# Moving seven of 31 convolution taps and the head norms' roots from VectorE to ScalarE and GpSimd in a hybrid decoder block

## The chip, the cores and the metric

The kernel runs on one core of a Trainium2 chip. The metric is the device time of one execution in microseconds (us), the median of several runs. A core has a matrix engine (TensorE, PE in the profile; its weight loads are PEld), a vector engine (VectorE, DVE), an activation engine (ScalarE, ACT), a general engine (GpSimd, POOL) and a queue that only starts transfers (SyncE, SP). Each engine works through its own list of instructions strictly in order and waits at semaphores for the others. SBUF is the working memory, PSUM the memory into which TensorE writes; GpSimd has no instruction here that touches PSUM.

## The reference, cut to what matters

One decoder layer over 512 tokens of width 1024, all in float32. Two token mixers run side by side on the same normed input, then comes an MLP:

```python
u = rms_norm(x, norm_mix_g)
proj = u @ w_in                          # q, k, v, glu (2 x 1024), two gates
q = rms_norm(q, q_norm_g) * HEAD_DIM ** -0.5      # 16 heads of 64
k = rms_norm(k, k_norm_g)                         # 4 heads of 64
attn = sliding_window_attention(q, k, v, attn_sinks, rel_bias) @ w_attn_o
h = a * sigmoid(gate)                    # the two halves of glu
h = causal_depthwise_conv(h, w_dw) + b_dw         # 31 taps, per channel
conv = silu(layer_norm(h)) @ w_conv_out
x = x + (sigmoid(gate_attn) * attn + sigmoid(gate_conv) * conv) @ w_out
x = x + square(relu(rms_norm(x, norm_mlp_g) @ w_ff1)) @ w_ff2
```

The window is 128 tokens, so a block of 128 queries sees its own and the previous block of keys. The convolution adds, for each of the 1024 channels, 31 shifted copies of a row of 512 tokens, each times a weight of that channel.

## The kernel before, in words

**Matrix products.** Every float32 product is made of three products of rounded halves: a matrix is split into a high part (ScalarE writes a rounded copy, `wh`, line 140) and a low part (the rest, `wl`, line 141). For the weights of the first half of the kernel GpSimd makes the low part, 128x1024 elements at a time.

**The stretch with the mixers.** `gemms()` (line 568) yields 80 steps: four times eight steps of `glu_pair` (the gate and value halves of the convolution input, lines 431 to 444, two tiles of 128 channels each) and four of `q_group` (the queries of four heads, line 473), then 32 steps for the two gates (`gates`, line 557). A step is one half of a weight tile's matrix products, or one block of 128 tokens of a query group. Between the steps a hand-written table (`stages`, lines 575 to 589) calls the attention pieces: `q_stage` transposes the scaled queries, `score_stage` makes the scores of four heads and their softmax, `prob_stage` transposes the probabilities, `value_stage` multiplies them with the values. The loop at line 598 also takes three convolution instructions per step from step 8 on (`CONV_STEP`, line 602); what is left at the end follows at line 614.

**Who orders.** Outside a short start the framework lists the instructions of each engine itself before the run: it goes by the order in which the program names them, and lets a later one pass when, by its own estimate of durations, an earlier one would still have to wait. On the chip that list is fixed.

**The convolution.** `conv_pair(c)` (line 446) works on two channel tiles. Their sums lie in two PSUM tiles (`cps`, tile name `cv`). All 31 taps of both are VectorE instructions on 128x512 elements: the first a product (line 455), the other 30 a product and a sum into the PSUM tile (line 457). Then VectorE adds the tile with its bias into `csum` (lines 463 and 465), and for the first three pairs ScalarE copies it out to SBUF with the bias (line 467). There are eight tiles, so 248 taps.

**The roots.** `q_group` copies the query block out of PSUM (ScalarE, line 258), squares it (line 260) and sums the squares of each head (VectorE, line 261). When its four blocks are done, `mean_eps` (line 131) and `rsqrt` (line 105) take 1/sqrt of 16 numbers per partition in 12 small VectorE instructions (lines 133, 110, 111 and three rounds of 113, 114 and 115). Line 486 then scales the queries on VectorE (both inputs in SBUF), line 487 rounds them on ScalarE, line 488 makes the low part on GpSimd, and only then can `q_stage` transpose them (line 498). The keys go the same way once, at the start (lines 401 to 416).

**What the attention pieces share.** `qtp` (line 496), `ptp` (line 535) and `op` (line 545) are PSUM tiles of one kind with two buffers, so TensorE can only write the next one when its readers are done with the one before the last: line 499 on ScalarE for `qtp`, 538 on ScalarE and 539 on VectorE for `ptp`, 552 on ScalarE and 554 on VectorE for `op`. Line 508 puts the sink column into the score tile on VectorE; line 518 adds the bias and takes the row minimum of the negated scores on VectorE; line 521 is the exponential on ScalarE; line 524 the reciprocal on VectorE; line 525 the scaling on GpSimd.

**After the stretch.** The low part of the attention output (`aTl`, line 612), the output projection with the layer norm of the convolution between its steps, the convolution's and the merged output projections, and the MLP, whose weights VectorE splits instead of GpSimd.

Of the kernel before, what the change touches and what calls it, by code (L numbers as in the profile page):

```python
# [42 lines left out]
START_ENGINES = {ENG.PE, ENG.DVE, ENG.Activation, ENG.Pool}  # L43
CONV_STEP = 3
LINE = 256
LEAD = 128
# [5 lines left out]
def tile_hybrid_block(  # L52
# [69 lines left out]
    def rsqrt_root(y, ms, w, tag):  # L122

        a = sm.tile([P, w], F32, name=f"a_{tag}", tag=f"a{w}")
        ve.reciprocal(y, y)
        ve.tensor_tensor(out=a, in0=y, in1=y, op=ALU.mult)
        ve.scalar_tensor_tensor(out=a, in0=a, scalar=-0.5, in1=ms, op0=ALU.mult, op1=ALU.mult)
        ve.scalar_tensor_tensor(out=y, in0=a, scalar=1.5, in1=y, op0=ALU.add, op1=ALU.mult)
        return y

# [269 lines left out]

    rk = rsqrt(mean_eps(ssk, HD, 16, "k"), 16, "k")
    k3 = kraw.rearrange("p t (g d) -> p (t g) d", d=HD)
# [28 lines left out]
    def glu_pair(c):  # L431
# [7 lines left out]
        for j, (wh, wl) in enumerate(stationary_tiles(w_in, V_END + 256 * c, 2, f"a{c}")):  # L439
# [4 lines left out]
                                    op0=ALU.add, op1=ALU.mult)  # L444

    def conv_pair(c):

        cts = (2 * c, 2 * c + 1)
        for ct in cts:
            cps[ct] = aux.tile([P, S], F32, name=f"cv_{ct}", tag="aux")  # L450
        for j in range(CW):
            for ct in cts:
                src, w = hh[ct][:, j:j + S], wcol[:, ct, j:j + 1]
                if j == 0:
                    ve.tensor_scalar(out=cps[ct], in0=src, scalar1=w, scalar2=None, op0=ALU.mult)
                else:
                    ve.scalar_tensor_tensor(out=cps[ct], in0=src, scalar=w, in1=cps[ct],  # L457
                                            op0=ALU.mult, op1=ALU.add)
                yield
        for ct in cts:  # L460
            b = wcol[:, ct, CW:CW + 1]
# [11 lines left out]
    def q_group(g):  # L473
# [3 lines left out]
        for t in range(NT):  # L477
# [23 lines left out]
    def score_stage(g, t):  # L501
# [5 lines left out]
        l4 = sm.tile([P, GRP], F32, name=f"l_{nm}", tag="l4")  # L507
        ve.tensor_copy(s4[:, :, 2 * P], nsink[:, GRP * g:GRP * g + GRP])
        for hp in range(2):
# [81 lines left out]
    def convs():  # L591
        for c in range(4):
            yield from conv_pair(c)

    conv = convs()
    last_stage = max(stages)
    ln = None
    for step, _ in enumerate(gemms()):
        for fn, args in stages.pop(step, []):
            fn(*args)  # L600
        if step >= 8:
            for _ in range(CONV_STEP):
                next(conv, None)
        if step == last_stage:
# [361 lines left out]
```

## Time and profile before

| | |
|---|---|
| time, median of 3 runs (lowest to highest) | 805.65 us (805.05 to 805.86) |
| the profiled execution's own time | 808.36 us |
| its span, from the first to the last instruction | 806.6 us |
| mean granted TensorE clock | 0.989 |
| DMA: moved, mean rate | 79.57 MB, 99 GB/s |
| the mixers' stretch, from the first convolution tap to the low part of the attention output | about 62 to 335 us of the span |

Times in the profile are microseconds from the start of the span unless marked ns. A row of groups has the line of the kernel, the engine, the operation, the tile it writes and those it reads, the shape, the count, then the busy time in all and the mean of one in ns, then the idle time in front. A row of waits reads "who waited, for whom: us in total, times, longest". A row of stretches has busy microseconds and instructions of each engine, then the granted TensorE clock as a share of full speed. Matrix products are pipelined, so their durations overlap and a busy TensorE is not one at its peak.

### The profile page before, as it was taken

Reading aid. Unit: us, or ns where it says so; the run is one execution under the profiler, and the core shown is the slowest. Engines: PE = TensorE matmul, PEld = TensorE weight load, DVE = VectorE, ACT = ScalarE, POOL = GpSimd, SP = SyncE. Lnnn points to the kernel's source line nnn. Section 1 sums busy time; section 2 is a strip of 40 time slices with the busy share of each in tenths; the row PEclk is TensorE's granted clock in tenths of the full one; section 3 lists DMA queues with packets and bytes.
Section 4 is the critical chain, followed back from the end, with each engine's and each line's share of the span. In section 5 each row is a group of like instructions: output and inputs, shape, how many; then the busy total and the mean of one; then the engine's idle time right before and its main releaser. Section 6 shows DMA issues by size and latency. Waiting matters only on the chain.

```text
span 806.6 us, 10416 instructions
## 1 busy us (share of the span) xinstructions
PE 781.7 (97%) x3960; PEld 662.8 (82%) x3960; DVE 629.4 (78%) x1046; ACT 378.8 (47%) x627; POOL 210.5 (26%) x108
## 2 busy tenths in 40 slices
PE   7999898998989999999999999999999999999998
PEld 7989796987968888787788889888888888888886
DVE  5539999999999999977983587687568756885683
ACT  5543255456565555244433436543554356435541
POOL 4343536344454443372357100000000000000000
PEclk8999999999999999999999999999999999999999
DMA  7421313213122213523134443333332332331002
GB/s 268 135 81 53 104 54 104 79 55 116 51 69 88 96 53 105 167 95 105 47 110 129 159 157 106 104 105 105 105 104 105 105 105 88 112 114 53 19 34 105
DMA packets 64808, 79.57 MB, mean 99 GB/s; under 512 B 2980, under 2 KB 52180, under 8 KB 64758
## 3 DMA queue, kind: packets, MB, share of 16 engines
q1 hardware_dynamic: 64758, 78.91, 29.7%
q8 instruction: 31, 0.51, 0.3%
q14 instruction: 19, 0.16, 0.1%
HBM read 76.78 MB, written 2.12 MB: 98 GB/s over the span
## 4 chain that ended last, share of the span: by engine, by line
PE 81%; DVE 14%; DMA 2%; issue 1%; POOL 1%; ACT 1%; SPq 0%; DVEq 0%; POOLq 0%; ACTq 0%
PE ps_f L175 7%; PE ps_f L176 7%; PE ps_f L174 7%; DVE cv L457 4%; PE ps_x L886 4%; PE ps_x L887 4%; PE ps_x L884 4%; PE ps_tc L422 2%; PE ps_tc L423 2%; PE ps_wo L182 2%; PE ps_wo L180 2%; PE ps_y L886 2%; PE ps_y L887 2%; PE ps_y L884 2%; PE ps_wo L181 2%; PE ps_tc L424 2%
## 5 line engine op out<-in xcount | busy, mean ns | idle before, releaser
L457 DVE SCALAR_TENSOR_TENSOR cv<-h,wcol,cv 128x512 f32<-128x512 f32 x240 | 167.2, 745 | 0.2
L175 PE MATMUL ps_f<-x2Tl,wh_f 128*128 128x512 f32 (+1 forms) x280 | 104.3, 373 | 0.4 <-DVE x2Tl L193 0.3
L174 PE MATMUL ps_f<-x2Th,wh_f 128*128 128x512 f32 (+1 forms) x280 | 103.7, 372 | 0.2 <-ACT x2Th L192 0.2
L176 PE MATMUL ps_f<-x2Th,wl_f 128*128 128x512 f32 (+1 forms) x280 | 103.9, 371 | 0.0
L141 DVE TENSOR_TENSOR wl_f<-raw_f,wh_f 128x1024 fp32r<-128x1024 f32 x32 | 39.1, 1224 | 57.8 <-ACT wh_f L140 56.6
L175 PEld LDWEIGHTS ps_f<-x2Tl,wh_f 128*128 128x128 f32 x280 | 52.7, 188 | 9.9 <-DVE x2Tl L193 0.9
L174 PEld LDWEIGHTS ps_f<-x2Th,wh_f 128*128 128x128 f32 x280 | 52.6, 188 | 9.5 <-ACT x2Th L192 0.5
L176 PEld LDWEIGHTS ps_f<-x2Th,wl_f 128*128 128x128 f32 x280 | 52.8, 188 | 9.0
L140 ACT CAST wh_f<-raw_f 128x1024 fp32r<-128x1024 f32 x32 | 33.6, 1054 | 54.6 <-PE ps_f L175 36.2
L794 DVE TENSOR_TENSOR wl_b<-b,wh_b 128x1024 fp32r<-128x1024 f32 x24 | 29.4, 1223 | 22.2 <-ACT wh_b L807 22.1
L525 POOL TENSOR_TENSOR s<-s,r 128x1024 f32<-128x1024 f32 (+1 forms) x16 | 26.9, 1680 | 68.5 <-DVE r L524 33.6
L807 ACT CAST wh_b<-b 128x1024 fp32r<-128x1024 f32 x24 | 25.3, 1055 | 40.5 <-PE ps_y L887 13.2
L807 ACT CAST wh_t<-t 128x1024 fp32r<-128x1024 f32 x24 | 24.9, 1053 | 36.8 <-DVE t L794 16.9
L521 ACT ACTIVATE s<-s,negm 128x257 f32<-128x257 f32 (+1 forms) x64 | 30.2, 476 | 22.5 <-DVE negm L518 13.4
L180 PE MATMUL ps_q<-wh_q,uTh 128*128 128x256 f32 x128 | 36.6, 286 | 0.0
L182 PE MATMUL ps_q<-wh_q,uTl 128*128 128x256 f32 x128 | 36.3, 283 | 0.0
L181 PE MATMUL ps_q<-wl_q,uTh 128*128 128x256 f32 x128 | 36.2, 283 | 0.0
L794 DVE TENSOR_TENSOR wl_t<-t,wh_t 128x1024 fp32r<-128x1024 f32 x24 | 29.0, 1220 | 5.9 <-ACT wh_t L807 5.4
L794 DVE TENSOR_TENSOR aSl<-ss,aSh 128x1024 fp32r<-128x1024 f32 x16 | 19.6, 1226 | 13.2 <-ACT aSh L820 13.2
L141 POOL TENSOR_TENSOR wl_wc<-raw_wc,wh_wc 128x1024 fp32r<-128x1024 f32 x8 | 19.9, 2493 | 32.8 <-ACT wh_wc L140 32.8
L141 POOL TENSOR_TENSOR wl_g<-raw_g,wh_g 128x1024 fp32r<-128x1024 f32 x8 | 20.0, 2511 | 31.0 <-ACT wh_g L140 31.0
L175 PE MATMUL ps_co<-sTl,wh_wc 128*128 128x512 f32 x64 | 25.0, 394 | 2.3 <-DVE sTl L682 2.3
(295 smaller groups left out, 2301.3 us busy)
## 6 DMA issues: line engine op xcount, KB each, us to landing
raw_f<-in_w_ff_dram SPq DMA_DIRECT2D x32, 512.0 KB, 4.2
b<-in_w_ff_dram SPq DMA_DIRECT2D x32, 512.0 KB, 4.1
x<-in_x_dram SPq DMA_DIRECT2D x8, 512.0 KB, 4.8
raw_g<-in_w_in_dram SPq DMA_DIRECT2D x8, 512.0 KB, 4.4
raw_a<-in_w_in_dram SPq DMA_DIRECT2D x8, 512.0 KB, 4.0
rawm_q<-in_w_in_dram SPq DMA_DIRECT2D x8, 512.0 KB, 3.5
raw_ta<-in_w_in_dram SPq DMA_DIRECT2D x8, 512.0 KB, 4.5
raw_tc<-in_w_in_dram SPq DMA_DIRECT2D x8, 512.0 KB, 3.5
```

The source lines that it names most:

```text
L141: lo_eng.tensor_tensor(out=wl, in0=raw_ap, in1=wh.bitcast(F32), op=ALU.subtract)
L174: pe.matmul(ps, wh[:, k, :], ah[:, k, cols], start=(k == 0), stop=False)
L175: pe.matmul(ps, wh[:, k, :], al[:, k, cols], start=False, stop=False)
L176: pe.matmul(ps, wl[:, k, :], ah[:, k, cols], start=False, stop=(k == nk - 1))
L180: pe.matmul(ps, ah, wh, start=first, stop=False)
L181: pe.matmul(ps, ah, wl, start=False, stop=False)
L182: pe.matmul(ps, al, wh, start=False, stop=last)
L457: ve.scalar_tensor_tensor(out=cps[ct], in0=src, scalar=w, in1=cps[ct], op0=ALU.mult, op1=ALU.add)
L794: ve.tensor_tensor(out=out, in0=a, in1=b, op=ALU.subtract)
L807: se.copy(wh, half)
L884: pe.matmul(banks[t], ah, wh[:, j, :], start=(first and h + j == 0), stop=False, skip_group_check=True)
L886: pe.matmul(banks[t], ah, wl[:, j, :], start=False, stop=False, skip_group_check=True)
```

## The change

- Of the 31 taps of a tile, the first seven (`SIDE`) leave VectorE. ScalarE multiplies the shifted row with its weight into SBUF (an Identity activation with the weight as scale); GpSimd adds the products into an SBUF tile `side`. The first tap of a tile writes `side` directly, so a tile has seven ScalarE instructions and six GpSimd additions. They are called after every third VectorE tap.
- VectorE makes the other 24 taps as before, and one new instruction per tile that adds `side` to the PSUM tile.
- The roots of the query and key norms are made by `rsqrt_pool`: 14 GpSimd instructions in place of 12 on VectorE.
- The sink column (line 508) is copied by ScalarE instead of VectorE.
- Per step the loop takes three convolution instructions in steps 8 to 19, then 2, 2 and 3 in turn up to the last attention step (73), then 4. A pair has 50 VectorE instructions to take instead of 62.

```diff
+SIDE = 7
...
+    def rsqrt_pool(ss, n, w, tag):
+
+        ms = sm.tile([P, w], F32, name=f"ms_{tag}", tag=f"ms{w}")
+        y = sm.tile([P, w], F32, name=f"y_{tag}", tag=f"y{w}")
+        a = sm.tile([P, w], F32, name=f"a_{tag}", tag=f"a{w}")
+        yi = y.bitcast(I32)
+        ge.tensor_scalar(out=ms, in0=ss, scalar1=1.0 / n, scalar2=EPS, op0=ALU.mult, op1=ALU.add)
+        ge.tensor_scalar(out=yi, in0=ms.bitcast(I32), scalar1=-0.5, scalar2=RSQRT_MAGIC, op0=ALU.mult, op1=ALU.add)
+        for _ in range(3):
+            ge.tensor_tensor(out=a, in0=y, in1=y, op=ALU.mult)
+            ge.tensor_tensor(out=a, in0=a, in1=ms, op=ALU.mult)
+            ge.tensor_scalar(out=a, in0=a, scalar1=-0.5, scalar2=1.5, op0=ALU.mult, op1=ALU.add)
+            ge.tensor_tensor(out=y, in0=a, in1=y, op=ALU.mult)
         return y
...
-    rk = rsqrt(mean_eps(ssk, HD, 16, "k"), 16, "k")
+    rk = rsqrt_pool(ssk, HD, 16, "k")
...
+    side = {}
+
+    def side_pair(c):
+
+        for j in range(SIDE):
+            for ct in (2 * c, 2 * c + 1):
+                src, w = hh[ct][:, j:j + S], wcol[:, ct, j:j + 1]
+                if j == 0:
+                    side[ct] = gpool.tile([P, S], F32, name=f"side_{ct}", tag="side", bufs=4)
+                    se.activation(side[ct], src, AF.Identity, scale=w)
+                else:
+                    tap = gpool.tile([P, S], F32, name=f"tap_{ct}_{j}", tag="tap", bufs=3)
+                    se.activation(tap, src, AF.Identity, scale=w)
+                    ge.tensor_tensor(out=side[ct], in0=side[ct], in1=tap, op=ALU.add)
+                yield
+
     def conv_pair(c):
 
         cts = (2 * c, 2 * c + 1)
+        sides = side_pair(c)
         for ct in cts:
             cps[ct] = aux.tile([P, S], F32, name=f"cv_{ct}", tag="aux")
-        for j in range(CW):
+        for i, j in enumerate(range(SIDE, CW)):
             for ct in cts:
+                if (2 * i + ct) % CONV_STEP == 0:
+                    next(sides, None)
                 src, w = hh[ct][:, j:j + S], wcol[:, ct, j:j + 1]
-                if j == 0:
+                if j == SIDE:
                     ve.tensor_scalar(out=cps[ct], in0=src, scalar1=w, scalar2=None, op0=ALU.mult)
...
+        for ct in cts:
+            ve.tensor_tensor(out=cps[ct], in0=side[ct], in1=cps[ct], op=ALU.add)
+            yield
...
-        rq = rsqrt(mean_eps(ssq, HD, 16, f"q{g}"), 16, f"q{g}")
+        rq = rsqrt_pool(ssq, HD, 16, f"q{g}")
...
-        ve.tensor_copy(s4[:, :, 2 * P], nsink[:, GRP * g:GRP * g + GRP])
+        se.copy(s4[:, :, 2 * P], nsink[:, GRP * g:GRP * g + GRP])
...
+    def taps_at(step):
+
+        if step < 20:
+            return 3 if step >= 8 else 0
+        return (2, 2, 3)[step % 3] if step <= last_stage else 4
+
...
-        if step >= 8:
-            for _ in range(CONV_STEP):
-                next(conv, None)
+        for _ in range(taps_at(step)):
+            next(conv, None)
```

More of the change, by code (lines that the diff above doesn't have):

```diff
@@ L128, in rsqrt_root @@
         ve.scalar_tensor_tensor(out=y, in0=a, scalar=1.5, in1=y, op0=ALU.add, op1=ALU.mult)
+        return y
+    def rsqrt_pool(ss, n, w, tag):
[10 more added lines that the diff above has]
+            ge.tensor_tensor(out=y, in0=a, in1=y, op=ALU.mult)
         return y
```

## The prediction

> **What bounds the kernel now.** I read the page first, for the engines.
>
> ```profile
> span 806.6 us, 10416 instructions
> PE 781.7 (97%) x3960; PEld 662.8 (82%) x3960; DVE 629.4 (78%) x1046; ACT 378.8 (47%) x627; POOL 210.5 (26%) x108
> ```
>
> TensorE is busy 97% of the span. The change doesn't touch its work, so all that it can gain is time in which TensorE stands or runs slowly. Second, the waits of TensorE alone:
>
> ```profile
> PE qtp L498 <- DVE attnT L554: 7.5, 3, 2.9
> PE qtp L498 <- POOL qs L488: 2.2, 1, 2.2
> PE op L550 <- DVE pTl L539: 0.8, 2, 0.5
> ```
>
> These are 7.5 + 2.2 + 0.8 = 10.5 us, all around the query transposes. Third, the stretches of the mixers, and three short spells inside them:
>
> ```profile
> 62.00:335.00 273.00, 261.60 (x1458) 225.74 (x1456) 263.50 (x538) 135.33 (x295) 126.58 (x58) 0.98 0.25 82
> 145.00:195.00 50.00, 47.06 (x285) 41.67 (x284) 48.81 (x112) 27.09 (x65) 23.32 (x11) 0.97 0.24 77
> 245.00:330.00 85.00, 84.98 (x420) 71.42 (x419) 80.59 (x165) 44.97 (x91) 37.34 (x17) 1.00 0.26 85
> 99.90:103.30 3.40, 3.40 (x15) 2.82 (x14) 3.40 (x7) 1.09 (x2) 2.03 (x1) 0.50 0.13 15
> 140.90:144.30 3.40, 3.11 (x13) 2.74 (x14) 3.37 (x6) 0.68 (x2) 2.41 (x2) 0.50 0.00 0
> 192.10:195.50 3.40, 3.40 (x14) 3.01 (x12) 3.40 (x7) 1.17 (x2) 0.85 (x1) 0.50 0.41 103
> ```
>
> After three of the waits the granted clock is 0.50 for 3.4 us. That costs 3 x 3.4 x (1 - 0.50) = 5.1 us more, and follows the waits. So 10.5 + 5.1 = 15.6 us of the span can go.
>
> The stretches also say which part of VectorE's work does it. From 245 to 330 VectorE is busy 80.59 of 85 us, with taps throughout, and TensorE loses nothing (84.98 of 85). From 145 to 195 TensorE loses 2.9 us. What the second has and the first hasn't is a query group with its roots. So, fourth, the instructions in order there, on VectorE, GpSimd and TensorE:
>
> ```profile
> 169.05 2.36 DVE L110 TENSOR_SCALAR y_q<-ms_q 128x16 int32<-128x16 int32 x1
> 176.30 1.54 DVE L113 TENSOR_TENSOR a_q<-y_q 128x16 f32<-128x16 f32 x1
> 177.76 0.74 DVE L457 SCALAR_TENSOR_TENSOR cv<-h,wcol,cv 128x512 f32<-128x512 f32 x1
> 178.42 1.78 DVE L114 SCALAR_TENSOR_TENSOR a_q<-a_q,ms_q 128x16 f32<-128x16 f32 x1
> 181.20 1.20 DVE L486 TENSOR_TENSOR qraw<-qraw,y_q 128x1024 f32<-128x1024 f32 x1
> 189.85 0.84 DVE L554 TENSOR_TENSOR attnT<-op,osb 64x256 f32<-64x256 f32 x2
> ```
>
> ```profile
> 168.98 2.40 POOL L141 TENSOR_TENSOR wl_a<-raw_a,wh_a 128x1024 fp32r<-128x1024 f32 x1 [0.57 <-ACT wh_a L140]
> 175.91 1.89 POOL L525 TENSOR_TENSOR s<-s,r 128x1024 f32<-128x1024 f32 x1 [4.54 <-DVE r L524]
> 177.77 2.40 POOL L141 TENSOR_TENSOR wl_a<-raw_a,wh_a 128x1024 fp32r<-128x1024 f32 x1
> ```
>
> ```profile
> 187.44 0.46 PE L498 MATMUL qtp<-ident_r,qs 128*128 128x128 f32 x4
> 190.84 0.51 PE L498 MATMUL qtp<-ident_r,qs 128*128 128x128 f32 x4 [2.94 <-DVE attnT L554]
> ```
>
> Each long root instruction ends with a GpSimd instruction: 169.05 + 2.36 = 171.41 beside 168.98 + 2.40 = 171.38; 177.84 beside 177.80; 180.20 beside 180.17. With GpSimd idle, at the keys, the same ones are short:
>
> ```profile
> 39.47 0.17 DVE L110 TENSOR_SCALAR y_k<-ms_k 128x16 int32<-128x16 int32 x1
> 41.77 1.22 DVE L403 TENSOR_TENSOR kraw<-kraw,y_k 128x1024 f32<-128x1024 f32 x1
> ```
>
> So GpSimd blocks the roots: 2.36 + 1.54 + 1.78 - 3 x 0.17 = 5.2 us in which VectorE stands in a list fixed beforehand. It comes late to the score pieces, then to `attnT` (189.85), whose PSUM buffer TensorE wants for the second four transposes (2.94 us). The path had 5.2 - 2.9 = 2.3 us to spare. The Trainium skill (SBUF — State Buffer, "SBUF: two separate sides") says that the interface VectorE shares with GpSimd is an exclusive lock held for a whole instruction, taken by VectorE instructions in a 2-port mode or with two SBUF inputs; the ends above agree.
>
> **The change part by part.** *Roots off VectorE.* The four query groups lie in the stretch. VectorE loses
>
> ```profile
> L110 DVE TENSOR_SCALAR y_q<-ms_q 128x16 int32<-128x16 int32 x4 | 8.8, 2191 | 0.0
> L114 DVE SCALAR_TENSOR_TENSOR a_q<-a_q,ms_q 128x16 f32<-128x16 f32 x12 | 7.3, 612 | 0.0
> L113 DVE TENSOR_TENSOR a_q<-y_q 128x16 f32<-128x16 f32 x12 | 6.5, 539 | 0.0
> L115 DVE SCALAR_TENSOR_TENSOR y_q<-a_q,y_q 128x16 f32<-128x16 f32 x12 | 3.3, 273 | 0.0
> L457 DVE SCALAR_TENSOR_TENSOR cv<-h,wcol,cv 128x512 f32<-128x512 f32 x228 | 159.3, 745 | 0.2
> ```
>
> 8.8 + 7.3 + 6.5 + 3.3 = 25.9 us of roots, and with them the 5.2 us lag per group. Line 486 stays on VectorE with two SBUF inputs and can still be blocked, at most as in the worst group:
>
> ```profile
> 129.84 2.83 DVE L486 TENSOR_TENSOR qraw<-qraw,y_q 128x1024 f32<-128x1024 f32 x1
> ```
>
> 2.83 - 1.22 = 1.6 us, below the 2.3 us to spare.
>
> *Taps off VectorE.* 56 taps at 0.745 us are 41.7 us; eight additions of `side` (taken as a tap, one SBUF input and PSUM) put back 6.0. VectorE's busy time in the stretch becomes 263.5 - 25.9 - 41.7 + 6.0 = 202 us. By the row of 245 to 330 taps cost TensorE nothing as such, so I count no gain for them, but they loosen the path: 2.33 instead of 3 are taken per step, and twelve steps lie between line 486 at 129.84 and at 181.20, 4.3 us each; the 20.8 us from 169.05 to 189.85 are 4.8 steps, so 4.8 x 0.67 x 0.745 = 2.4 us more to spare.
>
> *GpSimd gets* 48 additions of 128x512 and 14 small instructions per group. Rows:
>
> ```profile
> L657 POOL TENSOR_TENSOR vsum<-vsum,lsq 128x512 f32<-128x512 f32 x3 | 4.7, 1557 | 0.9 <-ACT lsq L656 0.9
> L525 POOL TENSOR_TENSOR s<-s,r 128x1024 f32<-128x1024 f32 x12 | 22.7, 1893 | 46.9 <-DVE r L524 26.1 <-PE ps_a L424 16.2 <-PE op L550 4.5
> L525 POOL TENSOR_TENSOR s<-s,r 128x512 f32<-128x512 f32 x4 | 4.2, 1040 | 21.5 <-PE ps_q L182 14.1 <-DVE r L524 7.5
> L436 POOL MEMSET h<- 128x30 f32 x8 | 0.5, 123 | 0.0
> ```
>
> The addition is the operation of line 657: 1.56 us, at least 2.40 / 2 = 1.20. So 48 x 1.56 = 75 us. No row shows a 16-column GpSimd arithmetic instruction. Its bounds are 0.12 (the memset) and 1.04 (512 columns). The line through the two rows of 525 falls 853 ns per 512 columns and leaves 0.19 us at none, 0.21 at 16: an estimate, and what I take, being nearest in size. 56 x 0.21 = 12 us, at the upper bound 58. GpSimd's busy time in the stretch becomes 126.6 + 75 + 12 = 213 us of the 261 that are left without the loss, at the upper bound 260. It is then nearly full, but not over.
>
> The skill (GPSIMD Engine Reference, "Engine selection") would leave element-by-element arithmetic to VectorE, GpSimd being about twice as slow with two inputs. The rows agree (1557 against 745 ns), but the price falls on an engine with room. The lock rule would let the 48 additions hold no tap, since a tap reads one tensor from SBUF; the tap at 177.76 took 0.74 us inside a GpSimd instruction, as the rule has it. Were taps held too, 202 + 75 = 277 us would pass the 261 by 16, and the stretch would end about where it does now.
>
> *ScalarE gets* 56 taps and the 16 sink copies, which are tiny. An Identity with a per-partition operand is
>
> ```profile
> L467 ACT ACTIVATE h<-cv,wcol 128x512 f32<-128x512 f32 x6 | 3.9, 698 | 1.7 <-DVE csum L465 1.7
> ```
>
> so 56 x 0.70 = 39 us: 135.3 + 39 = 174 of 261. The taps lie in one list with the copies that free PSUM for TensorE, so one of those can be 0.7 us later.
>
> *Keys.* GpSimd stands idle there, so 14 x 0.21 = 2.9 us replace 12 on VectorE, 11 of which took 41.77 - 39.47 = 2.3 us: about 0.4 us later (0.8 us earlier to 12 us later at the bounds). Cover:
>
> ```profile
> 45.79 2.00 ACT L408 CAST k2h<-kraw 128x1024 fp32r<-128x1024 f32 x2 [4.42 <-DVE s L508]
> 50.30 0.64 PE ktp_h L414 x8
> ```
>
> 50.30 - 47.79 = 2.5 us; I cost it at nothing. At the upper bound TensorE would wait some 9 us once.
>
> *New wait.* Line 486 on VectorE now waits for GpSimd's root, and all that is queued behind it on VectorE (taps, `pTl`, scores, `attnT`) waits too. The root starts behind at most one 2.4 us weight part and takes 2.9, done about 174, where now it is done at 181; I count no lag, but see the first rival.
>
> *Sum.* Removable 15.6 us. Left over, between nothing and all of it: I take one wait of 0.8 us, the size of the small row above, for each of the four groups, 3.2 us, because ScalarE and GpSimd are fuller. Gain 15.6 - 3.2 = 12.4 us. The profiled execution took 808.36 us in its own time, 1.8 us around the span of 806.6; its span would be 794.2 and its time 796.0. It lies 2.7 us above the median of the runs, 805.65; from the median 793.2.
>
> **The rivals.** *VectorE stands at line 486 for GpSimd's roots (slower).* With w us of standing, the wait per group is w + 1.6 - 2.3 - 2.4 = w - 3.1, and each brings 1.7 us of half clock: 4 x (w - 3.1) + 6.8 against the 15.6 that went. It decides at w = 5.3. GpSimd stands that long in its own list now, when the scaling of the scores is next:
>
> ```profile
> POOL s L525 <- PE ps_a L424: 16.2, 2, 8.2
> ```
>
> At w = 8.2 it is 27.2 - 15.6 = 11.6 us slower, 817.3. For it: that row, and unknown small instructions. Against: the framework puts the roots where its own estimates see GpSimd free, and VectorE late is what GpSimd mostly waits for. About w = 5.3 the time is unchanged, which is also what comes out if the transposes' waits have another cause.
>
> *ScalarE is the late one.* At the wait above it frees the first transposes' buffer only here:
>
> ```profile
> 189.72 0.58 ACT L499 CAST qT<-qtp 128x512 fp32r<-128x512 f32 x1
> ```
>
> 190.30 against TensorE's 187.90, 2.4 us, with no help from `attnT`. If its list stays late, with the taps in it, three waits of 2.4 and two half-clock spells (3.4) remain, and the gain is 15.6 - 10.6 = 5.0 us: 800.6. Against: ScalarE waited for scores of the late VectorE.
>
> **How the numbers follow.** The forecast, 788.5 to 797.5 (all of 15.6 gone, or half of it), has 0.62. ScalarE late, up to 803, has 0.15. Unchanged has 0.08, and VectorE standing, to 817, 0.15. The range reaches from just below all of 15.6, 788.0, to 805.0: it leaves out the slow rival and a little of the rest. Faster by over 0.2% (1.6 us, about what a measurement of this kernel can tell from no change) 0.77, within it 0.08, slower 0.15.
>
> **What would show it.** Right: no wait of `qtp` on `attnT` above 1 us, no spell at 0.50 between 95 and 200 us, TensorE over 98% busy from 62 to 320, short `y_q` instructions on GpSimd ending before 181 - 5 us in the second group, taps still at 745 ns, GpSimd near 80% busy. Wrong: VectorE idle before line 486 for GpSimd by more than 3 us, TensorE waiting on ScalarE's `qT` or `pTh`, `y_q` instructions near 1 us, ScalarE waiting at a tap for a free buffer.

## The result, and the profile after

The changed kernel takes 831.31 us (median of 4 runs, 827.62 to 832.25) where the kernel before took 805.75 us beside it (805.05 to 806.63): a ratio of 1.0308, with a 95% interval of 1.0275 to 1.0342. It is 25.6 us slower, and the forecast was 793.2 us, 788.0 to 805.0. The profiled execution has a span of 829.0 us against 806.6, 22.4 more; that is less than 25.6 because before's profiled execution lay 2.7 us above its median and after's 0.6 us below.

From here on line numbers are those of the kernel that a row comes from. The change shifts them: before's line 486 (the scaling of the queries) is 524 after, 487 is 525, 488 is 526, 437 (the gate's tanh) is 453, 443 is 459, 457 (a VectorE tap) is 492, 537 is 575, 554 (`attnT`) is 592. New are 471 and 474 (ScalarE's products), 475 (GpSimd's additions), 496 (VectorE's addition of `side`) and 138 to 144 (the roots on GpSimd).

First the page of the kernel after, span and engines:

```profile
span 829.0 us, 10497 instructions
PE 793.0 (96%) x3960; PEld 669.4 (81%) x3960; DVE 573.3 (69%) x922; ACT 415.0 (50%) x699; POOL 285.0 (34%) x226
```

VectorE is down by 629.4 - 573.3 = 56 us, and the kernel is longer. TensorE does the same 3960 products, yet it is busy 793.0 us instead of 781.7, 11.3 more, and idle 829.0 - 793.0 = 36.0 instead of 806.6 - 781.7 = 24.9, 11.1 more. Together that is the 22.4 us of span. The stretches show where both halves of it come from (columns as in the prediction: busy time of each engine, then the granted clock):

```profile
62.00:335.00 273.00, 250.06 (x1369) 214.75 (x1368) 214.50 (x436) 162.01 (x354) 188.65 (x159) 0.95 0.22 72
141.84:148.67 6.83, 6.18 (x15) 4.82 (x16) 6.71 (x17) 4.37 (x11) 6.83 (x4) 0.50 0.06 7
206.70:210.11 3.41, 3.41 (x13) 2.93 (x12) 3.41 (x6) 2.40 (x5) 1.78 (x2) 0.50 0.25 58
```

In the mixers' stretch TensorE is busy 250.06 of 273 us at a mean clock of 0.95, before 261.60 at 0.98. So TensorE waits more, and has more time at half clock: seven spells in the stretch, one of them of 6.83 us, where the kernel before had three of 3.4. The difference in clock is worth 273 x 0.03, some 8 us (an estimate), so over a third of the loss. The last group of gate products (before's line 422, after's 438; lowest, median and highest duration, then the first and the last start) dates the loss; the first row is of the kernel before, the second of the kernel after:

```profile
L422 PE MATMUL ps_tc<-uTh,wh_tc x64: 388/390/477, 279.0 to 328.8; 128*128 128x512 f32 x64
```

```profile
L438 PE MATMUL ps_tc<-uTh,wh_tc x64: 389/389/477, 300.2 to 349.9; 128*128 128x512 f32 x64
```

349.9 - 328.8 = 21.1 of the 22.4 us are lost before the mixers end. This date serves below as a measure of the stretch alone. Next the waits of TensorE, of VectorE and of ScalarE in the kernel after:

```profile
PE ps_a L438 <- ACT h L453: 6.5, 3, 4.9
PE qtp L536 <- DVE attnT L592: 5.1, 2, 2.9
PE ps_g L438 <- ACT sq L276: 2.6, 2, 1.9
PE ptp L575 <- ACT wh_g L156: 2.3, 1, 2.3
PE ptp L575 <- ACT wh_ta L156: 2.2, 1, 2.2
```

```profile
DVE qraw L524 <- POOL y_q L144: 23.3, 4, 8.1
```

```profile
ACT qs L525 <- DVE qraw L524: 33.3, 4, 8.9
ACT tap L474 <- POOL side L475: 8.8, 17, 0.7
```

The wait of `qtp` on `attnT`, which was to vanish, is still there with 5.1 us. The two waits of `ptp` have the same cause, although the profile names a weight cast: `ptp` shares its buffers with `op`, not with the weights. The second `attnT` ends at 178.80 and 233.12 us, and `ptp` starts at 178.94 and 233.27; that is the same 0.15 us as in the kernel before, where `attnT` ended at 190.69 and `qtp` started at 190.84. A weight cast only happened to end in between (178.86 and 233.19). So the waits on `attnT` are 9.6 us here, against 7.5 before. New are the waits for ScalarE's `h` and `sq`, 9.1 us. Behind them stand VectorE, 23.3 us at line 524 for GpSimd's roots, and ScalarE, 33.3 us at line 525 for that line 524, and 17 times at a tap for a free buffer. The first query group shows the chain as it happens: GpSimd, ScalarE, VectorE, TensorE in the order of the lists (start, duration, and in brackets the idle time before it with its releaser):

```profile
69.93 13.74 POOL L475 TENSOR_TENSOR side<-side,tap 128x512 f32<-128x512 f32 x11
83.63 2.40 POOL L157 TENSOR_TENSOR wl_g<-raw_g,wh_g 128x1024 fp32r<-128x1024 f32 x1
86.11 0.20 POOL L138 TENSOR_SCALAR ms_q<-ssq 128x16 f32<-128x16 f32 x1
86.40 2.40 POOL L157 TENSOR_TENSOR wl_a<-raw_a,wh_a 128x1024 fp32r<-128x1024 f32 x1
88.88 0.20 POOL L139 TENSOR_SCALAR y_q<-ms_q 128x16 int32<-128x16 int32 x1
89.16 0.22 POOL L141 TENSOR_TENSOR a_q<-y_q 128x16 f32<-128x16 f32 x1
92.43 0.22 POOL L144 TENSOR_TENSOR y_q<-a_q,y_q 128x16 f32<-128x16 f32 x1
92.61 2.34 POOL L157 TENSOR_TENSOR wl_a<-raw_a,wh_a 128x1024 fp32r<-128x1024 f32 x1
```

```profile
72.52 0.73 ACT L474 ACTIVATE tap<-h,wcol 128x512 f32<-128x512 f32 x1 [0.53 <-POOL side L475]
73.76 0.72 ACT L474 ACTIVATE tap<-h,wcol 128x512 f32<-128x512 f32 x1 [0.52 <-POOL side L475]
74.40 0.35 ACT L274 COPY qraw<-ps_q 128x256 f32<-128x256 f32 x1
96.12 1.04 ACT L525 CAST qs<-qraw 128x1024 fp32r<-128x1024 f32 x1 [7.86 <-DVE qraw L524]
97.07 0.59 ACT L453 ACTIVATE h<-ps_g 128x512 f32<-128x512 f32 x1
```

```profile
92.69 3.35 DVE L524 TENSOR_TENSOR qraw<-qraw,y_q 128x1024 f32<-128x1024 f32 x1 [7.28 <-POOL y_q L144]
```

```profile
97.72 0.80 PE L438 MATMUL ps_a<-uTh,wh_a 128*128 128x512 f32 x1 [4.88 <-ACT h L453]
```

Eleven additions stand in one row in GpSimd's list, then a weight part, the first root, another weight part, the other roots. VectorE waits 7.28 us for them, ScalarE 7.86 for VectorE, and behind ScalarE's line 525 stands the tanh of line 453, which frees the PSUM tile that TensorE wants: 4.88 us. That line 524 itself takes 3.35 us fits the weight part beside it, which ends at 94.95. This reading makes the order of GpSimd's list the culprit. The experiments show that it names only the smaller part.

The Trainium skill (PSUM — Partial Sum Buffer, "Engine vs sequencer instructions") says that the queues of ScalarE, VectorE and GpSimd are strictly first in, first out. The rows agree: TensorE's last product for the tanh ended at 92.84, and the tanh started at 97.07, as line 525 ended.

### The profile page after: what moved, and what is told of

Same layout as the page of the kernel before. It is cut to its first block, busy times and chain, and to the rows that moved or that the text cites. A ratio compares the mean times of both kernels' runs of the same rounds, so it can differ in the third digit from the quotient of the medians.

```text
span 829.0 us, 10497 instructions
## 1 busy us (share of the span) xinstructions
PE 793.0 (96%) x3960; PEld 669.4 (81%) x3960; DVE 573.3 (69%) x922; ACT 415.0 (50%) x699; POOL 285.0 (34%) x226
## 4 chain that ended last, share of the span: by engine, by line
PE 65%; DVE 11%; POOL 6%; ACT 4%; issue 2%; DMA 1%; SPq 0%; ACTq 0%; POOLq 0%; DVEq 0%
PE ps_f L191 7%; PE ps_f L192 7%; PE ps_f L190 7%; PE ps_x L930 4%; PE ps_x L927 4%; PE ps_x L929 3%; DVE cv L492 3%; POOL side L475 3%; PE ps_tc L439 2%; PE ps_tc L438 2%; PE ps_y L930 2%; PE ps_y L927 2%; PE ps_y L929 2%; PE ps_co L191 2%; PE ps_tc L440 2%
## 5 line engine op out<-in xcount | busy, mean ns | idle before, releaser
L492 DVE SCALAR_TENSOR_TENSOR cv<-h,wcol,cv 128x512 f32<-128x512 f32 x184 | 127.8, 745 | 0.3
L475 POOL TENSOR_TENSOR side<-side,tap 128x512 f32<-128x512 f32 x48 | 60.4, 1297 | 3.0 <-ACT tap L474 3.0
L850 ACT CAST wh_t<-t 128x1024 fp32r<-128x1024 f32 x24 | 24.9, 1051 | 35.7 <-DVE t L837 15.8
L474 ACT ACTIVATE tap<-h,wcol 128x512 f32<-128x512 f32 x48 | 33.5, 720 | 8.8 <-POOL side L475 8.8
L438 PE MATMUL ps_a<-uTh,wh_a 128*128 128x512 f32 x64 | 28.3, 442 | 6.5 <-ACT h L453 6.5
```

The source lines that it names most:

```text
L438: pe.matmul(ps, wh[:, k, :], ah[:, k, :], start=(k == 0), stop=False)
L475: ge.tensor_tensor(out=side[ct], in0=side[ct], in1=tap, op=ALU.add)
L850: se.copy(wh, half)
```

## The experiments

Each time stands with its ratio to the kernel before, measured beside it, and the 95% interval. Theories: A, the burst of additions ahead of the roots in GpSimd's list; B, the roots on GpSimd as such; C, ScalarE's added load; D, the thinner queue; E, ScalarE's products held by GpSimd's additions through three tap buffers; F, GpSimd's additions holding VectorE and GpSimd's own work; G and H, below, on what made the waits of the kernel before.

### The parts of the change

**The roots alone** (before, plus):

```diff
-    rk = rsqrt(mean_eps(ssk, HD, 16, "k"), 16, "k")
+    rk = rsqrt_pool(ssk, HD, 16, "k")
...
-        rq = rsqrt(mean_eps(ssq, HD, 16, f"q{g}"), 16, f"q{g}")
+        rq = rsqrt_pool(ssq, HD, 16, f"q{g}")
```

> The kernel before with one part of the change alone: the key and query roots on GpSimd, all taps on VectorE, three conv instructions per step. Theory A (order: the burst of side additions stands ahead of the roots in GpSimd's list, and VectorE then stands at the scaling of qraw by y_q): without additions the roots start behind one or two weight parts of 2.4 us, VectorE stands there under 3 us per group (23.3 us in four waits after the change), the half-clock spells of 3.4 us fall from seven to two at most, and the time is below the kernel before: 792 to 803 us. Theory B (fourteen small instructions one after the other on GpSimd make VectorE stand, whatever else GpSimd does): waits of 4 to 8 us at the scaling of qraw as after the change, and 812 to 831 us.

Measured: 810.7 us, 1.0058 [1.0039, 1.0078]. Slower by 4.7 us: a time between the two expectations, with VectorE's waits as theory B has them. VectorE's and then TensorE's waits of this kernel:

```profile
DVE qraw L501 <- POOL y_q L143: 18.0, 4, 5.0
```

```profile
PE qtp L513 <- DVE attnT L569: 8.8, 3, 2.9
PE ps_a L437 <- ACT h L452: 3.0, 1, 3.0
```

VectorE stands 4.5 us per group with no addition anywhere on GpSimd. That is close to the 5.2 us of lag that the prediction found per group in the kernel before: the stand took the lag's place. And the waits of `qtp` on `attnT` are 8.8 us, no less than 7.5, although no root instruction is left on VectorE. With a stand of the same length in the lag's place, this alone does not yet say whether the lag makes those waits.

**The taps alone** (after, with those two lines undone):

```diff
-    rk = rsqrt_pool(ssk, HD, 16, "k")
+    rk = rsqrt(mean_eps(ssk, HD, 16, "k"), 16, "k")
...
-        rq = rsqrt_pool(ssq, HD, 16, f"q{g}")
+        rq = rsqrt(mean_eps(ssq, HD, 16, f"q{g}"), 16, f"q{g}")
```

> The kernel after with the roots back on VectorE; taps of ScalarE and GpSimd, sink copies and queue as after the change. Theory B: VectorE no longer waits for GpSimd's roots, so the loss of 25.6 us is gone: 795 to 808 us. Theory A: GpSimd's additions come in the same bursts, and each held the short root instructions of VectorE as the weight parts do in the kernel before; a burst of ten is 13 us, so long y_q and a_q instructions add up to 5 to 10 us per group on VectorE: 808 to 825 us. A third theory (C: ScalarE's taps delay its copies out of PSUM) gives a time near after, 822 to 832 us, with TensorE's waits on ScalarE and short root instructions.

Measured: 823.6 us, 1.0215 [1.0183, 1.0246]. Theory B falls as the main cause; theories A and C both allowed this time. So the taps alone (with the sink copies and the thinner queue) cost 17.3 us and the roots alone 4.7, 22.0 of 25.6 together.

**The queue as before** (after, with):

```diff
-        if step < 20:
-            return 3 if step >= 8 else 0
-        return (2, 2, 3)[step % 3] if step <= last_stage else 4
+        return CONV_STEP if step >= 8 else 0
```

> The kernel after with one part undone: three conv instructions queued per step from step 8 on, as before. Theory D (the thinner queue moves the mixers' late parts and is to blame): the time comes back to within 5 us of the kernel before, 801 to 811 us. Theory A: the count per step hardly changes the bursts of side additions on GpSimd, VectorE still stands 3 us or more at the scaling of qraw in at least two of four groups: 822 to 840 us.

Measured: 832.4 us, 1.0325 [1.0289, 1.0362], as after. Theory D falls.

**The same work in another order** (after, plus order edges, which keep an instruction behind another in an engine's list without a wait):

```diff
-                    se.activation(tap, src, AF.Identity, scale=w)
-                    ge.tensor_tensor(out=side[ct], in0=side[ct], in1=tap, op=ALU.add)
+                    behind("ACT", se.activation(tap, src, AF.Identity, scale=w))
+                    behind("POOL", ge.tensor_tensor(out=side[ct], in0=side[ct], in1=tap, op=ALU.add))
```

> The kernel after with the same instructions on the same engines and another order: on GpSimd each side addition is kept behind the last weight part or root that the program issues ahead of it, on ScalarE each tap behind the last weight cast or square. Theory A: the roots no longer stand behind a burst, VectorE stands under 3 us per group at the scaling of qraw, and most of the loss of 25.6 us goes: 795 to 812 us. Theories B and C (the roots' own length, or ScalarE's load): the same work on the same engines, so 820 to 832 us as after.

Measured: 827.7 us, 1.0257 [1.0222, 1.0291]. Only 3.6 us under the kernel after, though the bursts were broken up. VectorE still stands 18.1 us at the scaling of `qraw`, as with the roots alone (18.0), so the bursts' part of that stand is gone; but it stands 22.0 us for `side` at the tile's end, which it did not before. This is a first sign against theory A, and a weak one, since the order brought a loss of its own.

### Which half of the side taps costs

These start from the taps alone, where the roots are on VectorE.

**Additions without products:**

```diff
-                    tap = gpool.tile([P, S], F32, name=f"tap_{ct}_{j}", tag="tap", bufs=3)
-                    se.activation(tap, src, AF.Identity, scale=w)
-                    ge.tensor_tensor(out=side[ct], in0=side[ct], in1=tap, op=ALU.add)
+                    ge.tensor_tensor(out=side[ct], in0=side[ct], in1=src, op=ALU.add)
```

> The taps alone (roots on VectorE) without ScalarE's 48 products: GpSimd adds the shifted rows of h unweighted, so this kernel leaves out the weights of taps 2 to 7 of each tile. GpSimd's load is that of the taps alone, ScalarE's is 34 us less, and nothing on ScalarE waits for a tap buffer. Theory E (GpSimd's additions come in bursts of 1.25 us each and hold ScalarE at its three tap buffers, so that the copies behind the taps that free PSUM come late): 806 to 816 us, without TensorE's waits on ScalarE's qraw copy (5.1 us there). Theory F (the bursts hold VectorE's roots and GpSimd's own scaling of the queries and scores): the loss stays, 819 to 827 us.

Measured: 806.7 us, 1.0009 [0.9991, 1.0027]. GpSimd still has its 48 additions,

```profile
L473 POOL TENSOR_TENSOR side<-side,h 128x512 f32<-128x512 f32 x48 | 55.7, 1160 | 3.1
```

and the whole 17 us are gone. Theory E fits. F falls as far as the additions' own time goes; where they stand in the list has changed as well (see below).

**Products without additions:**

```diff
                     se.activation(tap, src, AF.Identity, scale=w)
-                    ge.tensor_tensor(out=side[ct], in0=side[ct], in1=tap, op=ALU.add)
```

> The taps alone (roots on VectorE) without GpSimd's 48 additions: ScalarE makes all products, which are added to nothing, so this kernel leaves taps 2 to 7 of each tile out of the sum. Theories E and F both need the additions: without them ScalarE's taps run freely at 0.72 us and the time is 800 to 811 us. Theory C (the 39 us that ScalarE has more to do delay its copies by themselves): 816 to 826 us.

Measured: 807.9 us, 1.0029 [1.0006, 1.0052]. ScalarE has its 56 products and the kernel is 1.9 us slower than before: theory C falls. Each half costs next to nothing, both together 17 us. What the pair has and the halves lack is that one engine waits for the other. In the kernel with the taps alone, ScalarE stands 15 times at a tap for a buffer, and the end of such a row and what TensorE waited for then are these lines, of ScalarE, VectorE and TensorE:

```profile
168.41 0.72 ACT L474 ACTIVATE tap<-h,wcol 128x512 f32<-128x512 f32 x1 [0.53 <-POOL side L475]
170.91 0.72 ACT L474 ACTIVATE tap<-h,wcol 128x512 f32<-128x512 f32 x1 [0.53 <-POOL side L475]
173.08 1.32 ACT L474 ACTIVATE tap<-h,wcol 128x512 f32<-128x512 f32 x2
174.96 0.58 ACT L590 COPY osb<-op 64x512 f32<-64x512 f32 x1
```

```profile
175.96 0.84 DVE L592 TENSOR_TENSOR attnT<-op,osb 64x256 f32<-64x256 f32 x2
```

```profile
176.95 0.63 PE L575 MATMUL ptp<-ident,s 128*128 128x128 f32 x4 [2.52 <-ACT qraw L274]
```

The profile names `qraw`, but here too the buffer of `ptp` comes free with `attnT`: it ends at 176.80, 0.15 us before TensorE starts. TensorE had finished `op` at 171.13; ScalarE copied it only at 174.96, behind taps and the exponentials that they delayed. Without products the same copy follows TensorE at once:

```profile
164.36 0.58 ACT L588 COPY osb<-op 64x512 f32<-64x512 f32 x1 [0.27 <-PE op L586]
```

A product takes 0.72 us and an addition 1.25, so with three buffers ScalarE is soon held to GpSimd's pace, 0.53 us at each tap, and everything behind a tap in its list, here the copy of `op`, comes late.

ScalarE's pace need not be the whole of it. The additions without products also come earlier (their list shows eight rows of six, the first of the third pair at 146.5 us, where the taps alone have one at 153.9 and a row of nine at 163.3). And two waits that grew with the taps alone, `op` on `pTl` (4.3 us) and `qtp` on `qs` (4.4), end behind VectorE's list: in the first, ScalarE's half was done at 137.17 and `pTl` came at 143.11, behind roots and taps. So how much of the 17 us is ScalarE's pace and how much the order of the other lists was not separated. A run with more or fewer tap buffers would have told; there is none.

**Three side taps in place of seven:**

```diff
-SIDE = 7
+SIDE = 3
```

> The taps alone (roots on VectorE) with three side taps per tile in place of seven: 24 products and 16 additions, bursts a third as long. Theories E and F (the length of the bursts on GpSimd): the loss of 17.3 us falls to a third or less, 806 to 813 us. If a single late instruction per group were enough: 816 to 824 us.

Measured: 807.5 us, 1.0018 [1.0000, 1.0035]. The loss goes with the length of the rows, and faster than in proportion: four additions of twelve are left per pair of tiles, but 1.5 us of 17.3. With so short a row the three buffers do, and ScalarE no longer waits for GpSimd at a tap.

**Additions and roots on GpSimd, no products** (after, with):

```diff
-                    se.activation(tap, src, AF.Identity, scale=w)
-                    ge.tensor_tensor(out=side[ct], in0=side[ct], in1=tap, op=ALU.add)
+                    ge.tensor_tensor(out=side[ct], in0=side[ct], in1=src, op=ALU.add)
```

> The kernel after without ScalarE's 48 products: GpSimd adds the shifted rows of h unweighted, so this kernel leaves out the weights of taps 2 to 7 of each tile. GpSimd keeps additions and roots. Theory E (the loss comes from ScalarE held at its tap buffers by GpSimd's additions): 808 to 815 us, the cost of the roots alone (4.7 us) and little more, although bursts still stand ahead of roots. Theory A (the bursts ahead of the roots make VectorE stand, and that is the loss): 820 to 832 us with waits of over 15 us at the scaling of qraw.

Measured: 815.0 us, 1.0104 [1.0084, 1.0124]. GpSimd has all that the change gave it, VectorE stands as long as in the kernel after,

```profile
DVE qraw L522 <- POOL y_q L144: 21.4, 4, 7.8
```

and yet 16.3 us of the loss are gone. So theory A is not the main cause: the roots on GpSimd with that stand, which the first reading of the profile took for the cause, are worth 8.3 us here (815.0 - 806.7), and the products 16.3 (831.3 - 815.0), 16.9 with the roots on VectorE (823.6 - 806.7). The earlier place of the additions without products holds for this run too.

### What made the waits of the kernel before

The prediction put the waits of `qtp` on `attnT` down to the roots' lag. The trace of the kernel before shows another chain, here in the second query group, VectorE's lines first:

```profile
184.22 1.41 DVE L457 SCALAR_TENSOR_TENSOR cv<-h,wcol,cv 128x512 f32<-128x512 f32 x2
185.53 0.48 DVE L518 CUSTOM_DVE_ANT_0 s<-sp,bias,rb_sink 128x256 f32<-128x256 f32 x1
```

```profile
186.06 0.52 ACT L521 ACTIVATE s<-s,negm 128x257 f32<-128x257 f32 x1 [1.07 <-DVE negm L518]
188.16 0.58 ACT L552 COPY osb<-op 64x512 f32<-64x512 f32 x1
```

TensorE is done with `op` at 184.86, but ScalarE's copy of it is listed behind exponentials, these wait for VectorE's scores, and the scores stand behind taps.

**Sink copies and thinner queue alone** (before, with):

```diff
-        ve.tensor_copy(s4[:, :, 2 * P], nsink[:, GRP * g:GRP * g + GRP])
+        se.copy(s4[:, :, 2 * P], nsink[:, GRP * g:GRP * g + GRP])
...
-        if step >= 8:
-            for _ in range(CONV_STEP):
-                next(conv, None)
+        for _ in range(taps_at(step)):
+            next(conv, None)
```

> The kernel before with the two small parts of the change alone: the sink copies on ScalarE and the thinner queue of conv instructions; all taps and the roots stay on VectorE. The theory that came out of the roots alone: TensorE's wait for attnT at the second query transposes is not made by the roots but by the taps and sink copies listed ahead of the scores on VectorE (in the second group the scores were ready at 181.2 us and started at 187.1). Then fewer taps between the steps shorten those waits (8.8 us with the roots alone, 7.5 before), and the time is 796 to 805 us unless the taps that are left run past the mixers. The rival (the waits come from the roots' lag of 5.2 us): 804 to 808 us, the waits as before.

Measured: 804.0 us, 0.9984 [0.9961, 1.0008]: not to be told from no change. The waits of `qtp` on `attnT` were 7.1 us, nearly as before, so the run came out as the rival said. It does not settle the matter, since fewer taps per step don't take the taps from in front of the scores. Its mixers end 5.1 us earlier than before (323.7 for 328.8), but such dates compare one profiled execution with another. Before's lay 2.7 us above its median and had three half-clock spells in the stretch, this one had one, 1.7 us lost in each; the medians differ by 2.0:

```profile
L422 PE MATMUL ps_tc<-uTh,wh_tc x64: 388/389/477, 274.0 to 323.7; 128*128 128x512 f32 x64
```

**Taps behind `attnT`** (before, plus an order edge from each tap to the last `attnT`, and another count per step):

```diff
-            for _ in range(CONV_STEP):
+            n = (0, 6, 3)[step % 3] if 21 <= step <= last_stage else CONV_STEP
+            for _ in range(n):
...
+                    if "out" in gate:
+                        tc.add_manual_dep(
+                            tap.ins, gate["out"].ins.name,
```

> The kernel before with the same instructions and another order of VectorE's taps alone: from step 21 on no taps are queued in a score step and six in the step behind it, and every tap is kept behind the attnT that the program issued last. Theory G (the second query transposes wait because attnT, which frees their PSUM buffer, is listed behind scores that stand behind taps; the roots' lag does not make it): TensorE's waits of qtp on attnT fall from 7.5 us to under 2, the three half-clock spells go too, and the time is 793 to 801 us. Theory H (the roots' lag of 5.2 us per group makes it): the waits stay over 5 us, 803 to 809 us. If the taps come out too late for the layer norm, TensorE waits for them at 360 to 420 us instead.

Measured: 821.6 us, 1.0186 [1.0165, 1.0208]. The waits of `qtp` on `attnT` are gone to the last, although the roots' instructions still take 25.5 us on VectorE (27.7 before). So theory G holds as far as this: with the taps out of the way the lag does no harm. Its time failed, for another reason, TensorE's first two waits:

```profile
PE mu_ps L651 <- DVE csum L472: 12.6, 1, 12.6
PE op L557 <- DVE pTl L546: 7.8, 2, 4.0
```

**The same with sink copies on ScalarE and the thinner queue** (the kernel before last, plus the order edges, and):

```diff
-        return (2, 2, 3)[step % 3] if step <= last_stage else 4
+        return (0, 4, 3)[step % 3] if step <= last_stage else 4
```

> The kernel before with sink copies on ScalarE, the thinner queue (four and three conv instructions in two of three steps, none in the score step) and every tap behind the attnT issued last; taps and roots stay on VectorE. Theory G: waits of qtp on attnT under 2 us, 791 to 799 us, 2 us under the order alone. Theory H: as the thinner queue alone, 802 to 806 us.

Measured: 836.0 us, 1.0374 [1.0348, 1.0399]. Its first wait and its last gate products:

```profile
PE mu_ps L655 <- DVE csum L472: 35.8, 1, 35.8
```

```profile
L422 PE MATMUL ps_tc<-uTh,wh_tc x64: 389/390/477, 270.1 to 319.9; 128*128 128x512 f32 x64
```

This too is outside both expectations. The mixers end 328.8 - 319.9 = 8.9 us earlier than before, the most in any run; up to 2.7 of it is before's long profiled execution, and 5.1 came already with the sink copies and the thinner queue. The prediction had 15.6. Two waits of `qtp`, 2.1 us each, are left; the profile puts them down to weight casts, but they end 0.15 us behind `attnT` (183.39 and 231.23) like those above. Then TensorE stands 35.8 us, because the taps that were held back are not done when the layer norm wants their sums.

**The roots on GpSimd in that order** (taps behind `attnT`, counts (0, 6, 3), plus):

```diff
-        rq = rsqrt(mean_eps(ssq, HD, 16, f"q{g}"), 16, f"q{g}")
+        rq = rsqrt_pool(ssq, HD, 16, f"q{g}")
```

> The order of the taps behind attnT as in the first kernel of this call, with the key and query roots on GpSimd as well. If VectorE's stand at the scaling of qraw (18.0 us in four waits with the roots alone) is what the roots cost, it is there again and this kernel is 2 to 7 us slower than the one without; if GpSimd's roots only replace a lag of VectorE's own, within 2 us of it.

The keys' roots move as well. Measured: 820.4 us, 1.0167 [1.0138, 1.0195], within 2 us of the order without them: the stand (16.0 us) replaces the lag.

**Taps behind `attnT` at three places** (the first of these orders, sink copies on ScalarE, and):

```diff
-            n = (0, 6, 3)[step % 3] if 21 <= step <= last_stage else CONV_STEP
+            n = {26: 0, 27: 0, 28: 9, 38: 0, 39: 0, 40: 9, 50: 0, 51: 0, 52: 9}.get(step, CONV_STEP)
+            if n <= CONV_STEP:
+                gate.clear()
```

> The kernel before with sink copies on ScalarE, and with the taps kept behind attnT at the three value stages alone that stand ahead of the second query transposes; elsewhere three conv instructions per step as before. If the waits of qtp on attnT (7.5 us) and the half-clock spells behind them (3.4 us each, 1.7 us lost) are worth what the prediction counted, they go and nothing replaces them: 793 to 800 us. If holding VectorE's taps back costs the layer norm even at three places (TensorE's wait of mu_ps on csum, 12.6 us with all steps): 803 to 812 us.

Measured: 823.2 us, 1.0220 [1.0199, 1.0241], slower than both expectations. The waits of `qtp` on `attnT` are gone here too, but the nine taps that follow in a row bring 4.0 us of `op` on `attnT` and 3.6 on `pTl`, and `mu_ps` waits 11.4. Holding the taps at three places costs as much as at all.

**Three side taps and taps behind `attnT`** (the kernel with three side taps, plus the order edges, and):

```diff
-        return (2, 2, 3)[step % 3] if step <= last_stage else 4
+        return (0, 6, 3)[step % 3] if step <= last_stage else 4
```

> Three side taps per tile on ScalarE and GpSimd, sink copies on ScalarE, roots on VectorE, and every tap of VectorE kept behind the attnT issued last, as in the kernel whose last taps came 12.6 us late. The 24 taps that leave VectorE, less the eight additions that come back, are some 11 us: the wait of mu_ps falls to 0 to 4 us, qtp waits stay gone, 794 to 803 us. If the side taps' coupling takes it back: 806 to 815 us.

Measured: 802.5 us, 0.9962 [0.9947, 0.9978]: faster than both kernels, by 3.2 us than before. TensorE's waits in the stretch and its last gate products:

```profile
PE op L593 <- DVE pTl L582: 3.9, 2, 2.3
PE ps_ao L678 <- DVE aTl L660: 2.7, 1, 2.7
PE qtp L541 <- POOL qs L531: 2.6, 2, 2.2
```

```profile
L438 PE MATMUL ps_tc<-uTh,wh_tc x64: 389/389/476, 272.2 to 321.9; 128*128 128x512 f32 x64
```

The waits on `attnT` are gone, `mu_ps` no longer waits, and the mixers end 6.9 us earlier than before, up to 2.7 of them again before's long execution; 2.7 are given back at `aTl`. Beside the same kernel without the order (807.5) it is 5 us faster: here relief by side taps pays once the order uses it.

**Three side taps, three places** (the last kernel, and):

```diff
-        return (0, 6, 3)[step % 3] if step <= last_stage else 4
+        return {26: 0, 27: 0, 28: 9, 38: 0, 39: 0, 40: 9, 50: 0, 51: 0, 52: 9}.get(step, 3)
```

> Three side taps per tile on ScalarE and GpSimd, sink copies on ScalarE, roots on VectorE, taps kept behind attnT at the three places alone. If VectorE's relief by side taps is worth anything by itself, it is faster than the same order without side taps by 1 to 5 us; if TensorE does not wait for VectorE's taps elsewhere, equal to it or up to 3 us slower.

Measured: 812.5 us, 1.0081 [1.0065, 1.0097], 10.7 us faster than the same order without side taps, so the relief is worth more than expected there, and still slower than before.

## Why the prediction was wrong, step by step

**The prices were right.** In the kernel after:

```profile
L475 POOL TENSOR_TENSOR side<-side,tap 128x512 f32<-128x512 f32 x48 | 60.4, 1297 | 3.0 <-ACT tap L474 3.0
L474 ACT ACTIVATE tap<-h,wcol 128x512 f32<-128x512 f32 x48 | 33.5, 720 | 8.8 <-POOL side L475 8.8
L492 DVE SCALAR_TENSOR_TENSOR cv<-h,wcol,cv 128x512 f32<-128x512 f32 x184 | 127.8, 745 | 0.3
```

An addition took 1.30 us (forecast 1.56, at least 1.20), a product 0.72 (0.70), a VectorE tap 745 ns as before, so GpSimd's additions hold no tap, and a small root instruction 0.20 to 0.22 (0.21). The keys' scaling started 0.65 us later than before (42.42 for 41.77; forecast 0.4); no run shows its cost apart. Busy times over the whole kernel, too, came out near the forecast: VectorE lost 56 us (61.6 reckoned for the stretch), ScalarE gained 36 (39), GpSimd 75 (90 with the keys). None of this says when an instruction gets its turn.

**The step that failed most** is the sentence on ScalarE: "The taps lie in one list with the copies that free PSUM for TensorE, so one of those can be 0.7 us later." It priced one tap ahead of a copy. It missed that the taps wait for GpSimd: at 1.25 us an addition against 0.72 a product, three buffers fill up, and the list loses 0.53 us at every tap after that. In the row shown above the copy of `op` came 3.8 us after TensorE's last product. The pairing is worth 16.3 to 16.9 us by the runs with and without the products; how much of that is ScalarE's pace and how much the changed order of the lists stays open. The prediction named its sign ("ScalarE waiting at a tap for a free buffer"), but gave it no price and no place among the rivals; its second rival, a late ScalarE, was argued from the kernel before and ended at a gain.

**The new wait** was named and then counted at nothing: "The root starts behind at most one 2.4 us weight part and takes 2.9, done about 174 [...] I count no lag". The fourteen instructions take more than their durations: they follow each other every 0.28 to 0.31 us (thirteen from 88.88 to 92.65), which makes some 4.1 us for fourteen. With weight parts in between and additions ahead, VectorE stood 23.3 us in four groups, 5.8 each, and 4.5 with the roots alone. The first rival had this mechanism, and its sum does not do badly for the roots alone: without the 2.4 us that fewer taps give, it makes 4 x (4.5 - 0.7) + 6.8 - 15.6 = 6.4 us slower, against 4.7 measured. Where ScalarE has no products but the taps are off VectorE, it makes 0.2 us for the 5.35 us that VectorE stands per group, and 8.5 were measured against the kernel before; for the kernel after it makes 2.0 of the 25.6. So it was no price for the whole. Line 524 was also held longer than the bound of 2.83 us, 3.35 in the row of 92.69.

**The removable 15.6 us** were put down to GpSimd blocking the roots. The lag is real, but it doesn't make the waits by itself: with the taps out of the way they were nil, lag or not (the kernels of 821.6 and 820.4 us). Whether the waits would go with the lag alone is open, because the roots on GpSimd put a stand of 4.5 us in the place of 5.2, and the waits were 8.8 us. With that falls "taps cost TensorE nothing as such". It was read from a stretch without a query group, where no second transposes wait for `attnT`. The stretch got 8.9 us shorter at most, not 15.6.

The 5.1 us of half clock in that sum were no fixed price either. The kernel before took 803.26 us in a run with a mean clock of 0.997 and 808.03 in one with 0.989; the profiled execution had 0.989. A gain that includes its three spells can't be taken off the median in full, as the forecast did. The interval of 788.5 to 797.5 also has a slip: all of 15.6 us off the median is 790.1.

**What was right:** that VectorE's list is late ahead of `attnT`, that VectorE's relief can be turned into time, and, nearly, the price of each instruction. No run had the gain of 12.4 us; 3.2 us of it came with three side taps and the taps ordered behind `attnT`.

## What to carry to other kernels

When work moves to two engines that hand pieces to each other, price the pair: the faster one runs at the slower one's pace once the buffers between them are full, and everything behind it in its list comes late. A wait that a profile names is the last link only, and at times not even that: check that the named instruction touches the buffer that is waited for. Before the cause is put down to the engine that is late there, list what stands ahead of the late instruction in its engine's own order, and test by moving just that. Relief of an engine off the critical path was worth nothing here until the order let the urgent instructions use it, and the order that holds work back was worth nothing without such relief; the two were 807.5 and 821.6 us alone and 802.5 together.

The Trainium skill (Perfetto Trace Analysis, "Optimizing Scalar/DVE Operations") says that moving work from a saturated VectorE to ScalarE or even GpSimd may make sense. The runs agree with the "may": seven side taps cost 17.3 us, three nothing that matters, and three with the right order gained 3.2.

## What the runs showed of the hardware

Dependent GpSimd instructions on 128x16 elements last 0.20 to 0.22 us in the profile, but start 0.28 to 0.31 us apart (rows from 88.88 on above). An addition of 128x512 with two SBUF inputs on GpSimd lasts 1.30 us, and eleven in a row take 13.74 us, 1.25 each; 48 of them left VectorE's taps, one input from SBUF and one from PSUM, at 745 ns. After a wait of TensorE of 2.9 us the granted clock was 0.50 for 3.41 us (206.70 to 210.11), and with two waits close together (2.23 us up to 139.78, 1.16 us up to 142.49) for 6.83 us (141.84 to 148.67). Not every such wait was followed by half clock: the wait before 240.71 in the kernel before (2.28 us) and, in the kernel with products alone, the one of 2.94 us before 237.50 have a clock of 1.00 from their start to 245.20 and 241.30. So equal waits do not cost the same in every place or run.
